# Two-pass matmul order inside a weight chunk: all leading-bit matmuls before the trailing-bit ones

## The chip, the cores and the metric

The kernel runs on one core of a Trainium2 chip. The metric is the time of one execution on the device, in microseconds, as the median over several runs. Besides this time there is one profiled execution with a trace, whose instructions can be read one by one.

## The reference

Two transformer blocks with batch 1, 256 tokens and model width 2048, in float32. Cut to what matters here, they are a chain of large matrix products with small attention, convolution and normalisation steps between them:

```python
# first block (16 meta tokens are put in front: 272 rows)
proj = rmsnorm(h, g_pre_mix) @ w_in            # 2048 -> 5382
y    = concat(fox_attention, diff_attention, conv_branch)
h    = h + rmsnorm(y @ w_out, g_post_mix)
g    = causal_dwconv(hn @ w_gate, w_conv)      # 2048 -> 5632
h    = h + rmsnorm((silu(g) * (hn @ w_up)) @ w_down, g_post_ffn)
# second block (256 rows)
z    = rms_norm(r, g_mix) @ w_in               # 2048 -> 10240
y_conv = (c_b * causal_depthwise_conv(c_c * c_x, w_conv)) @ w_conv_out
r    = r + (sigmoid(g_a) * (attn @ w_attn_out) + sigmoid(g_c) * y_conv) @ w_o
r    = r + square(relu(rms_norm(r, g_mlp) @ w_up)) @ w_down    # 2048 -> 8192 -> 2048
r    = r + sigmoid(rms_norm(r, g_ple) @ w_ple_gate) * (p @ w_ple_proj)
```

## The kernel before

Every float32 operand is split into a leading part (rounded to the matmul's short float format) and a trailing part (the rest). A product of two operands is then three short products: leading x leading, leading x trailing and trailing x leading. Activations `xs` hold both parts side by side, so that a weight tile's leading part `wh` can meet both activation parts in one matmul of 512 columns when there are 256 tokens (`both` in the code, the line of `o2`, L250). With 258 or 272 tokens two matmuls are needed for it (L252 and L253). The trailing part `wl` of the weight tile meets only the leading activations (L254, 256 to 272 columns). Below, a matmul with `wh` is called a leading matmul and one with `wl` a trailing matmul.

`chunks` (L226) walks over one product's weights. A group is `nt` blocks of 128 output columns (mostly 4), each summed up in a PSUM bank of its own over all rows of the weight. The rows come in chunks of `ck` blocks of 128 rows (4 when `nt` is 4): a chunk is one DMA of 1 MB into a `wst` buffer (3 of these), and two halves, each split by ScalarE into a `wh` tile (L158, 4 buffers) and by VectorE into a `wl` tile (L159, 3 buffers). A chunk with `nt` = 4 has 16 leading and 16 trailing matmuls. In a group's last chunk the loop goes bank by bank, and after a bank's last matmul `evac` reads the bank out: into SBUF, or added to a sum there.

The split of chunk n+1 is written ahead of the matmuls of chunk n (`queue`, `sync`). The instructions of each engine are then put into their final order by the tile framework's scheduler, with semaphores for the dependencies; on the chip each engine takes its own instructions in that order. Since there are three `wl` buffers and two per chunk, the second `wl` of chunk n+1 goes into the buffer of the first `wl` of chunk n, and waits until that one has been read for the last time.

The deque `mm` holds the banks that groups take in turn: four at first, then 5 or 6 (`N.banks(5)`, `N.banks(6)`). With six, a group's third bank is the first bank of the group before, and its fourth the second one. The read-outs that the prediction speaks of are: `evac_r` (L1163) and `evac_f_` (L974), two VectorE additions from the bank for each bank (L1168, L1169; L981, L982), after every group of the two down products and of `w_o`; `total` (L301), a ScalarE copy and a VectorE addition (L303, L304), after up, gate and input products; and `evac_cb` (L1109), `total` and seven more VectorE operations (L1117 to L1121 and a split).

Of the kernel before, what the change touches and what calls it, by code (L numbers as in the profile page):

```python
# [16 lines left out]
P = 128  # L17
# [29 lines left out]
class Net:  # L47
# [178 lines left out]
    def chunks(self, W, c0, nt, rows, xs, n, evac, x0=0, ahead=None, ck=None, merge=True):  # L226


        nc = self.nc
        both = merge and 2 * n <= 512  # L230
        cols = nt * P
        ck = ck or 2048 // cols
        nk = len(rows)
        ps = []

        def use(parts, done, c):
            if not ps:
                ps.extend(self.bank(self.mm) for _ in range(nt))
            last = done + c == nk
            for k, j in [(k, j) for j in range(nt) for k in range(c)] if last else [(k, j) for k in range(c) for j in range(nt)]:  # L240
                wh, wl, i = parts[k]
                kk = done + k
                a = rows[kk][1]
                s = slice(j * P, (j + 1) * P)
                o = ps[j][:, :n]
                st, sp = kk == 0, kk == nk - 1
                xh = xs[:, a, 0, x0:x0 + n]
                if both:
                    o2 = ps[j].rearrange("p (s n) -> p s n", s=2)[:, :, :n]
                    nc.tensor.matmul(o2, wh[:, i, s], xs[:, a, :, x0:x0 + n], start=st, stop=False)  # L250
                else:
                    nc.tensor.matmul(o, wh[:, i, s], xh, start=st, stop=False)  # L252
                    nc.tensor.matmul(o, wh[:, i, s], xs[:, a, 1, x0:x0 + n], start=False, stop=False)  # L253
                nc.tensor.matmul(o, wl[:, i, s], xh, start=False, stop=sp)  # L254
                if last and k == c - 1:
                    evac(j, o, ps[j][:, 256:256 + n] if both else None)

        done = 0
        while done < nk:
            c = min(ck, nk - done)  # L260
            while rows[done + c - 1][0] - rows[done][0] != c - 1:
                c -= 1
            w = ahead.popleft() if ahead else self.load(W, rows[done][0], c, c0, cols)
            hk = max(1, 1024 // cols)
            parts = []
            for k0 in range(0, c, hk):
                kn = min(hk, c - k0)
                wh, wl = self.split_w(w[:, k0:k0 + kn])
                parts += [(wh, wl, i) for i in range(kn)]
            yield lambda parts=parts, done=done, c=c: use(parts, done, c)  # L270
            done += c
# [1000 lines left out]
```

## Time and profile before

| what | value |
|---|---|
| time, median of 3 runs | 2668.92 us (2668.3 to 2670.02) |
| time of the profiled execution | 2666.8 us |
| its span, first to last instruction | 2665.1 us |
| TensorE busy | 2642.2 us, 99% |
| VectorE busy | 1880.6 us, 71% |
| ScalarE busy | 1308.6 us, 49% |
| DMA, share of 16 engines | about 55% on the weights' queue |
| granted TensorE clock | 1.0 of full speed over the whole span |

The span lies 1.7 us below the time of the same execution, and that execution 2.1 us below the median. A matmul's own duration in the trace includes its way through the array, which overlaps with the next matmul; how fast matmuls follow one another is read from the distance of their starts.

### The profile page before, as it was taken

How to read it: one execution, taken by the hardware profiler on the slowest of the kernel's cores; microseconds unless marked ns; L12 is line 12 of the kernel's file. 1: busy time of each engine (PE TensorE's matmuls, PEld its weight loads, DVE VectorE, ACT ScalarE, POOL GpSimd, SP SyncE). 2: the span in 40 equal slices, each digit the busy share in tenths (PEclk: the TensorE clock that was granted, in tenths of full speed). 3: DMA queues.
4: the chain of work that ended last, by engine and by line, in shares of the span. 5: the costliest groups of instructions: out<-in, count | busy, mean ns of one | idle time of the engine just before them, and what ended most of it. 6: DMA issues, size and time to landing. Idle time of an engine off the chain costs nothing.

```text
span 2665.1 us, 41518 instructions
## 1 busy us (share of the span) xinstructions
PE 2642.2 (99%) x16542; PEld 2368.7 (89%) x16542; DVE 1880.6 (71%) x3460; ACT 1308.6 (49%) x2018; POOL 23.4 (1%) x49
## 2 busy tenths in 40 slices
PE   8999999999999999999999999999999999999999
PEld 8999999999898989888888888888888888888887
DVE  5897878866767676778766766666666666666684
ACT  5454555554444444456554555554544444444463
POOL 2000000000000000000000000000000000000000
PEclk9999999999999999999999999999999999999999
DMA  6644446555555555556445555555655665556564
GB/s 211 181 148 143 131 137 199 180 183 189 190 190 188 179 188 189 178 176 204 154 160 179 177 185 189 190 190 177 191 192 191 188 190 192 190 188 190 193 216 152
DMA packets 275586, 483.63 MB, mean 181 GB/s; under 512 B 8528, under 2 KB 75025, under 8 KB 275248
## 3 DMA queue, kind: packets, MB, share of 16 engines
q1 hardware_dynamic: 272560, 475.83, 55.0%
q8 instruction: 130, 2.13, 0.3%
q0 software_dynamic: 1680, 3.18, 0.3%
q10 hardware_dynamic: 1152, 1.97, 0.2%
q14 instruction: 64, 0.52, 0.1%
HBM read 476.74 MB, written 4.20 MB: 180 GB/s over the span
## 4 chain that ended last, share of the span: by engine, by line
PE 97%; DVE 2%; DMA 0%; issue 0%; ACT 0%; SPq 0%; DVEq 0%; ACTq 0%
PE ps L250 45%; PE ps L254 31%; PE ps L252 8%; PE ps L253 7%; PE ps L288 1%; PE ps L289 1%; PE ps L287 1%; DVE wl L159 1%; PE ps L633 1%; PE ps L619 0%; PE ps L626 0%; DMA tok<-in_x_dram 0%; PE ps L723 0%; PE ps L1052 0%; PE ps L661 0%
## 5 line engine op out<-in xcount | busy, mean ns | idle before, releaser
L159 DVE TENSOR_TENSOR wl<-w,wh 128x1024 fp32r<-128x1024 f32 x898 | 1095.8, 1221 | 549.4 <-PE ps L254 491.3
L158 ACT ACTIVATE wh<-w 128x1024 fp32r<-128x1024 f32 x898 | 945.3, 1059 | 1039.2 <-PE ps L250 702.4
L254 PE MATMUL ps<-x,wl 128*128 128x256 f32 (+2 forms) x4400 | 1235.2, 282 | 3.5 <-DVE wl L159 3.4
L250 PE MATMUL ps<-x,wh 128*128 128x512 f32 x3008 | 1058.1, 396 | 2.9 <-DVE x L162 2.3
L254 PEld LDWEIGHTS ps<-x,wl 128*128 128x128 f32 x4400 | 831.3, 189 | 7.1 <-DVE wl L159 6.1
L250 PEld LDWEIGHTS ps<-x,wh 128*128 128x128 f32 x3008 | 563.7, 188 | 133.3 <-DVE x L162 2.5
L250 PE MATMUL ps<-hid,wh 128*128 128x512 f32 x1728 | 599.9, 391 | 0.0
L254 PE MATMUL ps<-hid,wl 128*128 128x256 f32 x1728 | 483.8, 280 | 0.0
L252 PE MATMUL ps<-x,wh 128*128 128x258 f32 (+1 forms) x1392 | 400.1, 288 | 1.8 <-ACT x L161 1.8
L253 PE MATMUL ps<-x,wh 128*128 128x258 f32 (+1 forms) x1392 | 399.0, 287 | 0.0
L250 PEld LDWEIGHTS ps<-hid,wh 128*128 128x128 f32 x1728 | 323.2, 187 | 70.8
L254 PEld LDWEIGHTS ps<-hid,wl 128*128 128x128 f32 x1728 | 326.5, 189 | 0.3
L252 PEld LDWEIGHTS ps<-x,wh 128*128 128x128 f32 x1392 | 262.4, 189 | 4.2 <-ACT x L161 2.0
L253 PEld LDWEIGHTS ps<-x,wh 128*128 128x128 f32 x1392 | 264.1, 190 | 0.6 <-DVE x L162 0.2
L254 PE MATMUL ps<-y,wl 128*128 128x258 f32 (+1 forms) x512 | 144.3, 283 | 0.8 <-DVE wl L159 0.8
L304 DVE TENSOR_TENSOR t<-ps,t 128x256 f32<-128x256 f32 x160 | 67.6, 422 | 44.8 <-ACT t L303 43.6
L254 PEld LDWEIGHTS ps<-y,wl 128*128 128x128 f32 x512 | 97.0, 190 | 1.9 <-DVE wl L159 1.0
L250 PE MATMUL ps<-y,wh 128*128 128x512 f32 x256 | 90.9, 399 | 0.0
L250 PE MATMUL ps<-m,wh 128*128 128x512 f32 x256 | 90.5, 399 | 0.0
L303 ACT ACTIVATE t<-ps 128x256 f32<-128x256 f32 x160 | 60.3, 377 | 59.2 <-PE ps L254 59.2
L1168 DVE TENSOR_TENSOR h<-ps,h 128x256 f32<-128x256 f32 x144 | 61.0, 423 | 36.9 <-PE ps L254 34.0
L491 DVE SCALAR_TENSOR_TENSOR scr<-scr,par 128x258 f32<-128x258 f32 x180 | 82.5, 479 | 1.2
(255 smaller groups left out, 2037.7 us busy)
## 6 DMA issues: line engine op xcount, KB each, us to landing
w<-in_w_in_dram SPq DMA_DIRECT2D x117, 1024.0 KB, 5.2
w<-in_w_down_dram SPq DMA_DIRECT2D x108, 1024.0 KB, 5.1
w<-in_w_up_dram SPq DMA_DIRECT2D x106, 1024.0 KB, 5.5
w<-in_w_gate_dram SPq DMA_DIRECT2D x44, 1024.0 KB, 5.2
w<-in_w_o_dram SPq DMA_DIRECT2D x16, 1024.0 KB, 5.1
w<-in_w_ple_gate_dram SPq DMA_DIRECT2D x16, 1024.0 KB, 5.3
w<-in_w_out_dram SPq DMA_DIRECT2D x12, 1024.0 KB, 5.1
w<-in_w_attn_out_dram SPq DMA_DIRECT2D x8, 1024.0 KB, 5.0
```

Of the source, the lines that this page charges most:

```text
L158: nc.scalar.activation(hi, src, AF.Copy)
L159: return nc.vector.tensor_tensor(lo, src, hi.bitcast(F32), ALU.subtract)
L250: nc.tensor.matmul(o2, wh[:, i, s], xs[:, a, :, x0:x0 + n], start=st, stop=False)
L252: nc.tensor.matmul(o, wh[:, i, s], xh, start=st, stop=False)
L253: nc.tensor.matmul(o, wh[:, i, s], xs[:, a, 1, x0:x0 + n], start=False, stop=False)
L254: nc.tensor.matmul(o, wl[:, i, s], xh, start=False, stop=sp)
L287: self.nc.tensor.matmul(ps[b], xh, wh[:, j], start=k == 0, stop=False)
L288: self.nc.tensor.matmul(ps[b], xh, wl[:, j], start=False, stop=False)
L303: self.nc.scalar.activation(out, b, AF.Copy)
L304: self.nc.vector.tensor_tensor(out, a, out, ALU.add)
L491: V.scalar_tensor_tensor(cv[:, c], src, wdw_col(k, c), cv[:, c], ALU.mult, ALU.add)
L1168: V.tensor_tensor(r[:, i], ps2, r[:, i], ALU.add)
```

## The change

Within a chunk the loop is cut in two. First all leading matmuls of the chunk run, always row block by row block with the banks inside. Then all trailing matmuls run, in the same order, or, in a group's last chunk, bank by bank with the read-out behind each bank. Number, shapes and operands of the matmuls stay as they are, and so do buffers, banks, splits and loads. `gemm_rows` and the attention's own matmuls are not touched.

```diff
             last = done + c == nk
-            for k, j in [(k, j) for j in range(nt) for k in range(c)] if last else [(k, j) for k in range(c) for j in range(nt)]:
-                wh, wl, i = parts[k]
+
+            order = [(k, j) for k in range(c) for j in range(nt)]
+            for k, j in order:
+                wh, _, i = parts[k]
                 kk = done + k
                 a = rows[kk][1]
-                s = slice(j * P, (j + 1) * P)
-                o = ps[j][:, :n]
-                st, sp = kk == 0, kk == nk - 1
-                xh = xs[:, a, 0, x0:x0 + n]
+                lhs = wh[:, i, j * P:(j + 1) * P]
                 if both:
                     o2 = ps[j].rearrange("p (s n) -> p s n", s=2)[:, :, :n]
-                    nc.tensor.matmul(o2, wh[:, i, s], xs[:, a, :, x0:x0 + n], start=st, stop=False)
+                    nc.tensor.matmul(o2, lhs, xs[:, a, :, x0:x0 + n], start=kk == 0, stop=False)
                 else:
-                    nc.tensor.matmul(o, wh[:, i, s], xh, start=st, stop=False)
-                    nc.tensor.matmul(o, wh[:, i, s], xs[:, a, 1, x0:x0 + n], start=False, stop=False)
-                nc.tensor.matmul(o, wl[:, i, s], xh, start=False, stop=sp)
+                    o = ps[j][:, :n]
+                    nc.tensor.matmul(o, lhs, xs[:, a, 0, x0:x0 + n], start=kk == 0, stop=False)
+                    nc.tensor.matmul(o, lhs, xs[:, a, 1, x0:x0 + n], start=False, stop=False)
+            for k, j in [(k, j) for j in range(nt) for k in range(c)] if last else order:
+                _, wl, i = parts[k]
+                kk = done + k
+                o = ps[j][:, :n]
+                nc.tensor.matmul(o, wl[:, i, j * P:(j + 1) * P], xs[:, rows[kk][1], 0, x0:x0 + n], start=False, stop=kk == nk - 1)
                 if last and k == c - 1:
                     evac(j, o, ps[j][:, 256:256 + n] if both else None)
```

The scheduler answers to the new order, also on engines whose code is unchanged. The first place is TensorE between two groups of the last down product. `ps3488` to `ps3491` are the banks of the ending group, `ps3502` to `ps3505` those of the next; `ps3504` lies in the bank of `ps3488`, `ps3505` in that of `ps3489`. Before:

```order
L250 MATMUL ps3491_22700<-hid3001_19332,wh3486_22693 128x512
L254 MATMUL ps3491_22700<-hid3001_19332,wl3487_22694 128x256
L250 MATMUL ps3502_22793<-hid3001_19332,wh3493_22735 128x512 [waits Activation_49]
L254 MATMUL ps3502_22793<-hid3001_19332,wl3494_22736 128x256 [waits DVE_49]
L250 MATMUL ps3503_22794<-hid3001_19332,wh3493_22735 128x512 [waits PE_49]
L254 MATMUL ps3503_22794<-hid3001_19332,wl3494_22736 128x256
L250 MATMUL ps3504_22795<-hid3001_19332,wh3493_22735 128x512 [waits DVE_49,PE_49]
L254 MATMUL ps3504_22795<-hid3001_19332,wl3494_22736 128x256
L250 MATMUL ps3505_22796<-hid3001_19332,wh3493_22735 128x512 [waits DVE_49,PE_49]
```

The same place of the change:

```order
L258 MATMUL ps3491_22700<-hid3001_19332,wl3485_22690 128x256 x2
L258 MATMUL ps3491_22700<-hid3001_19332,wl3487_22694 128x256 x2
L249 MATMUL ps3502_22793<-hid3001_19332,wh3493_22735 128x512 [waits Activation_49]
L249 MATMUL ps3503_22794<-hid3001_19332,wh3493_22735 128x512 [waits PE_49]
L249 MATMUL ps3504_22795<-hid3001_19332,wh3493_22735 128x512 [waits DVE_49,PE_49]
L249 MATMUL ps3502_22793<-hid3001_19332,wh3493_22735 128x512
L249 MATMUL ps3503_22794<-hid3001_19332,wh3493_22735 128x512
L249 MATMUL ps3504_22795<-hid3001_19332,wh3493_22735 128x512
L249 MATMUL ps3502_22793<-hid3001_19332,wh3495_22739 128x512 [waits Activation_49]
L249 MATMUL ps3505_22796<-hid3001_19332,wh3493_22735 128x512 [waits DVE_49,PE_49]
```

Before, the fourth bank's first matmul is the seventh of the new group; now it is the eighth, behind seven leading matmuls, since the scheduler has put three others ahead of it. The last trailing matmul with `wl3485`, the ending chunk's first `wl`, is now the third from the chunk's end.

The second place is VectorE at the same boundary. `wl3494` and `wl3496` are the two trailing halves of the next group's first chunk, and `wl3496` goes into the buffer of `wl3485`. Before:

```order
L159 TENSOR_TENSOR wl3494_22736<-w3492_22733,wh3493_22735 128x1024 [waits DMAHW5_49,PE_49,Activation_49]
L1168 TENSOR_TENSOR h_135<-ps3488_22697,h_135 128x256 [waits PE_49]
L1169 TENSOR_TENSOR h_135<-ps3488_22697,h_135 128x256 [waits DVE_49]
L1168 TENSOR_TENSOR h_135<-ps3489_22698,h_135 128x256 [waits PE_49]
L1169 TENSOR_TENSOR h_135<-ps3489_22698,h_135 128x256 [waits DVE_49]
L1168 TENSOR_TENSOR h_135<-ps3490_22699,h_135 128x256 [waits PE_49]
L1169 TENSOR_TENSOR h_135<-ps3490_22699,h_135 128x256 [waits DVE_49]
L159 TENSOR_TENSOR wl3496_22740<-w3492_22733,wh3495_22739 128x1024 [waits PE_49,Activation_49]
L1168 TENSOR_TENSOR h_135<-ps3491_22700,h_135 128x256 [waits PE_49]
```

The same place of the change:

```order
L159 TENSOR_TENSOR wl3494_22736<-w3492_22733,wh3493_22735 128x1024 [waits DMAHW5_49,PE_49,Activation_49]
L1172 TENSOR_TENSOR h_135<-ps3488_22697,h_135 128x256 [waits PE_49]
L1172 TENSOR_TENSOR h_135<-ps3489_22698,h_135 128x256 [waits PE_49]
L1173 TENSOR_TENSOR h_135<-ps3488_22697,h_135 128x256 [waits DVE_49]
L159 TENSOR_TENSOR wl3496_22740<-w3492_22733,wh3495_22739 128x1024 [waits PE_49,Activation_49]
L1173 TENSOR_TENSOR h_135<-ps3489_22698,h_135 128x256 [waits DVE_49]
L1172 TENSOR_TENSOR h_135<-ps3490_22699,h_135 128x256
L1172 TENSOR_TENSOR h_135<-ps3491_22700,h_135 128x256 [waits PE_49]
```

Before, the read-outs of three banks stand ahead of the waiting split `wl3496`; now the second bank's last read (`L1173` of `ps3489`) stands behind it.

The third place is VectorE after the first `evac_cb` group of the convolution. `wl2424` is the second trailing half of the next group's first chunk, `wl2435` and `wl2437` those of its second chunk. The piece of the change, with 19 rows left out:

```order
L159 TENSOR_TENSOR wl2424_15430<-w2420_15423,wh2423_15429 128x1024 [waits DVE_49,PE_49]
L1123 SCALAR_TENSOR_TENSOR t2426_15456<-scr2286_14701,par_106,t2426_15456 128x256 [waits DVE_49]
...
L1123 SCALAR_TENSOR_TENSOR t2432_15501<-scr2286_14701,par_106,t2432_15501 128x256 [waits DVE_49]
L159 TENSOR_TENSOR wl2435_15512<-w2433_15509,wh2434_15511 128x1024 [waits DMAHW4_49]
L159 TENSOR_TENSOR y1944_13068<-t2430_15486,y1944_13068 128x256 [waits Activation_49]
L1124 TENSOR_TENSOR t2432_15501<-t2432_15501,rB1939_13045 128x256 [waits DVE_49]
L159 TENSOR_TENSOR wl2437_15516<-w2433_15509,wh2436_15515 128x1024 [waits PE_49]
```

Between `wl2424` and `wl2435` stand 21 instructions now, and 15 before.

## Rows read from the trace of the kernel before

**Rows 1.** Page, parts 1 and 4: busy time, and the chain by line.

```profile
PE 2642.2 (99%) x16542; PEld 2368.7 (89%) x16542; DVE 1880.6 (71%) x3460; ACT 1308.6 (49%) x2018; POOL 23.4 (1%) x49
PE ps L250 45%; PE ps L254 31%; PE ps L252 8%; PE ps L253 7%; PE ps L288 1%; PE ps L289 1%; PE ps L287 1%; DVE wl L159 1%; PE ps L633 1%; PE ps L619 0%; PE ps L626 0%; DMA tok<-in_x_dram 0%; PE ps L723 0%; PE ps L1052 0%; PE ps L661 0%
```

**Rows 2.** Page, part 5: leading matmuls of 512 columns; xcount | busy, mean ns | idle.

```profile
L250 PE MATMUL ps<-x,wh 128*128 128x512 f32 x3008 | 1058.1, 396 | 2.9 <-DVE x L162 2.3
L250 PE MATMUL ps<-hid,wh 128*128 128x512 f32 x1728 | 599.9, 391 | 0.0
```

**Rows 3.** Who TensorE waited for: total us, times, longest us.

```profile
PE ps L254 <- DVE wl L159: 4.1, 5, 1.4
```

**Rows 4.** Busy time by stretch; in brackets the count of instructions.

```profile
1440.00:1860.00 420.00, 418.64 (x2370) 362.61 (x2369) 276.31 (x417) 211.66 (x308) 0.00 (x0) 1.00 0.56 184
1880.00:2560.00 680.00, 680.00 (x3925) 599.57 (x3924) 465.55 (x701) 328.11 (x455) 0.00 (x0) 1.00 0.60 192
```

**Rows 5.** Timeline of TensorE, `gemm_rows`: start us, duration us (17 rows between).

```profile
2629.83 0.39 PE L288 MATMUL ps<-wl,x 128*128 128x512 f32 x1
...
2633.91 0.39 PE L288 MATMUL ps<-wl,x 128*128 128x512 f32 x1
```

**Rows 6.** Timeline of TensorE, matmuls of 256 columns (9 rows between).

```profile
425.55 0.28 PE L829 MATMUL ps<-wl,pl 128*128 128x256 f32 x1
...
426.74 0.28 PE L830 MATMUL ps<-wh,pl 128*128 128x256 f32 x1
```

**Rows 7.** Timeline of TensorE where 512-column matmuls follow pairs (6 rows between).

```profile
2568.16 0.28 PE L254 MATMUL ps<-hid,wl 128*128 128x256 f32 x1
2568.28 0.39 PE L287 MATMUL ps<-wh,x 128*128 128x512 f32 x1
...
2569.90 0.40 PE L288 MATMUL ps<-wl,x 128*128 128x512 f32 x1
```

**Rows 8.** Timeline of TensorE, runs of one kind in the touched loop.

```profile
1203.86 1.58 PE L250 MATMUL ps<-x,wh 128*128 128x512 f32 x6
...
1496.32 1.08 PE L250 MATMUL ps<-x,wh 128*128 128x512 f32 x4
1498.76 0.74 PE L254 MATMUL ps<-x,wl 128*128 128x256 f32 x4 [1.36 <-DVE wl L159]
```

**Rows 9.** Timeline of TensorE and VectorE, a matmul and the read-out it releases.

```profile
2134.14 0.28 PE L254 MATMUL ps<-hid,wl 128*128 128x256 f32 x1
...
2134.45 0.42 DVE L1168 TENSOR_TENSOR h<-ps,h 128x256 f32<-128x256 f32 x1 [0.50 <-PE ps L254]
2134.91 0.43 DVE L1169 TENSOR_TENSOR h<-ps,h 128x256 f32<-128x256 f32 x1
```

**Rows 10.** Timeline of TensorE and VectorE, a matmul and the split it releases.

```profile
2085.60 0.28 PE L254 MATMUL ps<-x,wl 128*128 128x256 f32 x1
...
2085.98 1.23 DVE L159 TENSOR_TENSOR wl<-w,wh 128x1024 fp32r<-128x1024 f32 x1 [1.53 <-PE ps L254]
```

**Rows 11.** Timeline of VectorE, splits and read-outs after one another.

```profile
2135.25 1.22 DVE L159 TENSOR_TENSOR wl<-w,wh 128x1024 fp32r<-128x1024 f32 x1
2136.39 0.42 DVE L1168 TENSOR_TENSOR h<-ps,h 128x256 f32<-128x256 f32 x1
2136.72 1.22 DVE L159 TENSOR_TENSOR wl<-w,wh 128x1024 fp32r<-128x1024 f32 x1
```

**Rows 12.** Timeline of VectorE and the weight loads (PEld): a late split.

```profile
1497.49 1.22 DVE L159 TENSOR_TENSOR wl<-w,wh 128x1024 fp32r<-128x1024 f32 x1
...
1498.76 0.54 PEld L254 LDWEIGHTS ps<-x,wl 128*128 128x128 f32 x4 [1.79 <-DVE wl L159]
```

**Rows 13.** Timeline of VectorE after the first `evac_cb` group; and TensorE there.

```profile
1425.69 0.42 DVE L159 TENSOR_TENSOR y<-t,y 128x256 fp32r<-128x256 f32 x1
...
1430.88 1.21 DVE L159 TENSOR_TENSOR wl<-w,wh 128x1024 fp32r<-128x1024 f32 x1
...
1432.14 0.74 PE L254 MATMUL ps<-x,wl 128*128 128x256 f32 x4 [0.53 <-DVE wl L159]
```

## The prediction

> **What bounds the kernel now.** I read the page first. TensorE is busy for 2642.2 of 2665.1 us, and the chain of work that ended last lies on it for 97%, almost all in the touched loop [rows 1]. VectorE and ScalarE have room on average, so a change of order on TensorE can move the time in three ways only: by how closely matmuls follow each other, by the waits of TensorE that exist, and by waits that it makes. The list of waits shows how few there are: the trailing matmuls waited five times for a late VectorE split, 4.1 us in all [rows 3]. Then I looked at the rhythm, by stretches without other work on TensorE. From 1880 to 2560 us 3925 matmuls take 680 us, 0.3465 us for a pair of a leading and a trailing one; from 1440 to 1860 it is 2370 in 420 us, of which 1.4 is a wait, so 0.3533 a pair [rows 4, 8]. The granted clock is 1.00, the 2.4 GHz level, in both [rows 4]. So the same pair has two rhythms, 0.0068 us apart, and the slower one costs 1185 x 0.0068 = 8 us in that stretch alone.
>
> **The change, term by term.** No matmul, weight load, split or transfer is added or removed. What moves is the order on TensorE and, through the scheduler, that of VectorE.
>
> *Rhythm.* In a row, 512-column matmuls follow at (2633.91 - 2629.83)/18 = 0.2267 us [rows 5] and 256-column ones at (426.74 - 425.55)/10 = 0.119 us [rows 6]. Sixteen of each, a chunk of four banks, take 3.63 + 1.90 = 5.53 us, as the fast rhythm does (16 x 0.3465 = 5.54) and 0.12 us less than the slow one. That is the gain if rows of one kind always run so: 8 us, and I allow 2 more for stretches that I did not separate. Against it stands that a row of 512-column matmuls that follows pairs does not start at this rhythm: its first seven steps take 1.62 us, 0.231 each, 0.033 us more than seven at 0.2267 [rows 7]. The touched loop has 5248 such pairs (3008 and 1728 [rows 2] and 512 with other operands by the code), that is 328 chunks, so a start like this in each would cost 328 x 0.033 = 11 us. The short runs of leading matmuls that the loop has already say both: six at (1.58 - 0.40)/5 = 0.236, four at (1.08 - 0.40)/3 = 0.227 [rows 8]. Bounds: -10 and +11. I take -5: the run that touched the slow stretch came at 0.227, and the start's price falls mostly where now the fast rhythm rules.
>
> *Five late splits.* Leading matmuls now give 3.63 us of cover before a chunk's first trailing one. That is more than the longest of the five waits, 1.4 us [rows 3]. Three go: 4.1 less the two after `evac_cb`, 0.53 and 1.36 [rows 13, 8], which I cost below, -2.2 us.
>
> *Banks at a group's end.* The four banks of a group used to finish 4 pairs apart, 1.39 us; now four trailing matmuls apart, 0.48 us, all in the last 1.9 us of the chunk. I walk one boundary of the last down product with the order above; zero is the end of the group's last matmul slot. The last reader of the ending chunk's first `wl` starts three slots earlier, at -0.36. A split starts 0.38 after the start of the matmul that releases it (2085.60 to 2085.98 [rows 10]): at +0.02. The instruction behind it starts 1.14 later (2135.25 to 2136.39 [rows 11]): the second bank's last addition at +1.16, and it ends 0.42 later [rows 9] at +1.58. A weight load that waited for VectorE starts 0.05 after its end (1497.49 + 1.22 = 1498.71 to 1498.76 [rows 12]): +1.63. The matmul that needs this bank stands behind seven leading ones, at 7 x 0.2267 = +1.59. Its weight load would start 0.12 earlier to keep the rhythm, at +1.47: 0.16 us late. The wait holds up every matmul behind it, so it is on the path. Groups with two additions as read-out are 20 of the first down product, 32 of the second and 4 of `w_o` by the code; I count 54 boundaries, +8 us. After groups read out by `total` the matmul stands behind nine (2.04) and the read-out comes one operation later (+1.16 + 0.33 + 0.42 + 0.05 = +1.96 against 1.92): 0.04 us at some 30 places, +1.5 with the few gate products that are shorter. Behind gate groups both banks are read ahead of the split: nothing. These prices hang on tenths of a microsecond: if the walk is 0.16 too slow it is 0 (and no gain, since these banks are not waited for now); if it is 0.16 too fast, it is +22.
>
> A rule bears on this term. The Trainium skill, page "TensorE: Matmul & The Clock Gate", part 2, says that TensorE pulls weight loads ahead of matmuls still in flight. By it the load would already lie in the array when the bank comes free, the loss would shrink from 0.16 to 0.04 a boundary, and the term from 8 to 2 us. The row speaks against it: the weight load starts only when VectorE is done, and its matmul with it [rows 12].
>
> *Convolution.* After an `evac_cb` group VectorE has 21 instructions between two splits, 15 before; the 15 took 1430.88 - 1425.69 = 5.19, 0.346 each [rows 13]. From the waiting split at +0.02: 1.14 + 21 x 0.346 = the next split at +8.4, its end at +9.6. The second chunk's trailing matmuls come at 5.54 + 3.63 = +9.2, their load at 9.05: 0.6 late, and the other half, three instructions later, is 0.8 late again. Two groups at 1.4 make 2.8 against 1.9 now, +1; and some 1 us for bank waits at the four other groups with five banks, worked out as above. Together +2, from 0 to +5.
>
> *Ends of stages.* Where a stage ends on its last read-out, the fourth bank's is released at the same moment as now, but three others stand close ahead of it. At most three additions of 0.34 us at four places, +4; I take 0, since the read-outs that I walked keep up but for the split between them.
>
> *Sum.* -5 - 2.2 + 8 + 1.5 + 2 = +4.3 us. The profiled execution took 2666.8 us; the median of the runs is 2668.92, and I add to it: 2673 us.
>
> **Rivals.**
>
> *The rhythm comes back in full and the banks come in time* (faster). One mechanism: rows of one kind lock at 0.2267 and 0.119 from their first matmul, -10, and the slots in which the scheduler put the fourth bank's matmul hold. For it: a long row runs without any deviation [rows 5]. It decides if the walk is 0.1 us too slow. With the late splits 2669 - 10 - 2 = 2657 us, or 2653 if the convolution gains too.
>
> *Banks cost more and each run pays its start* (slower). The start of 0.033 in each chunk is +11, banks at 0.3 us a boundary +16: 2669 + 11 + 16 - 2 = 2694 at its end, 2680 with half of it. For it: the run of six at 0.236 [rows 8], and a boundary that has no slack in the walk. Against: 256-column rows step at 0.119, a trifle below 0.120, which may give some back [rows 6].
>
> *Nothing visible happens.* The rhythm keeps its two levels in the new order, and the scheduler's slots cover the banks: 2669 - 2 = 2667 us. That the order itself stays as it was is excluded by the rows of the order above. The skill's rule on loads pulled ahead, with the rhythm unchanged, would end here too: 2669 + 2 + 2 - 2 = 2671.
>
> **How the numbers follow.** Of this kernel a measurement can tell about 0.2%, 5.3 us, from no change: 2663.6 to 2674.3. The forecast has 0.45, with its own range of 2665 to 2681, so that it lies about half below and half above the upper bound; the faster rival 0.20, the slower one 0.25, nothing visible 0.10. Faster by over 0.2%: the faster rival and a little of the forecast, 0.22. Within: half of the forecast, nothing visible and some of the slower rival, 0.36. Slower: 0.42. The range reaches from the faster rival's 2656 to 2688, between the two values of the slower one.
>
> **What would show it.** Right: no wait of trailing matmuls for splits but after `evac_cb`; waits of leading matmuls for VectorE's second addition, some fifty of 0.1 to 0.2 us; the stretch of `w_o` and the products before it nearer to 0.3465 us a pair than to 0.3533. Wrong: the last down product at 0.3465 with no such waits (banks in time), or a stretch without waits slower than 0.3533 a pair (the start of each run is dear). A third case would be VectorE splits late on a chunk's leading side, which I have excluded since ScalarE's `wh` buffers come free earlier than now.

## The result, and the profile of the changed kernel

| | kernel before | changed kernel |
|---|---|---|
| median of 6 runs each, taken side by side, us | 2668.61 (2661.26 to 2670.02) | 2682.44 (2678.85 to 2686.14) |
| ratio, 95% interval | | 1.0055 [1.0045, 1.0065] |
| span of the profiled execution, us | 2665.1 | 2682.5 |
| its own time, us | 2666.8 | 2684.47 |

The change costs 13.8 us by the medians, a ratio of 1.0055. That is above what a measurement here can tell from no change, and the kernel is slower, the way that was forecast; the forecast time, 2673, is 9 us short.

The page of the changed kernel, parts 1 and 4, answers to [rows 1]: TensorE has the same 16542 matmuls and is the chain as before.

```profile
PE 2655.5 (99%) x16542; PEld 2375.5 (89%) x16542; DVE 1824.6 (68%) x3460; ACT 1306.9 (49%) x2020; POOL 23.3 (1%) x49
...
PE ps L249 44%; PE ps L258 28%; PE ps L252 6%; PE ps L253 6%; PE ps L292 1%; PE ps L293 1%; PE ps L291 1%; DVE wl L159 1%; DMA w<-in_w_out_dram 1%; PE ps L637 1%; ACT wh L158 0%; PE ps L623 0%; PE ps L630 0%; DVE rB L863 0%; DMA w<-in_w_up_dram 0%
```

The list of waits of TensorE in the changed kernel (total us, times, longest us) answers to [rows 3]:

```profile
PE ps L343 <- DVE rB L863: 3.0, 2, 1.8
...
PE ps L252 <- DVE m L870: 2.6, 1, 2.6
...
PE ps L258 <- DVE wl L159: 2.2, 4, 0.6
```

The trailing matmuls (now L258) wait four times for a late split, 2.2 us, and all four follow `evac_cb` groups. Waits for `rB`, the last sum at the end of a stage, are 3.0 us; in the list of the kernel before they are 0.5:

```profile
PE ps L339 <- DVE rB L859: 0.5, 1, 0.5
```

The wait of 2.6 us (L252) is taken up below.

The same stretches as in [rows 4], busy time and in brackets the count of instructions (a count has some two matmuls in it that began ahead of the stretch):

```profile
1440.00:1860.00 420.00, 417.85 (x2393) 366.15 (x2392) 270.72 (x430) 209.44 (x308) 0.00 (x0) 1.00 0.56 188
1880.00:2560.00 680.00, 680.00 (x3876) 592.68 (x3876) 432.49 (x673) 321.61 (x443) 0.00 (x0) 1.00 0.59 190
```

From 1880 to 2560 us there are now 3876 matmuls, where there were 3925; from 1440 to 1860 us 2393, where there were 2370. So the change gained where pairs were slow and lost more where they were fast. Both kernels have 16542 matmuls, so the start of the k-th one can be compared across traces. This table gives by how many us each kernel's profiled execution falls behind that of the kernel before within each stretch (stretches by the times of before, the last 95 us left out; the kernels of the last five columns are described below):

| stretch, us | what runs there | changed | pairs in the last chunk | 7 banks | 4 `wl`, 3 `wh` | mixed | before, four more times |
|---|---|---|---|---|---|---|---|
| 0 to 387 | first block's attention | +0.5 | +1.4 | +0.5 | -0.6 | -0.6 | -0.8 to +0.4 |
| 387 to 480 | `w_out`, stage end | +7.5 | +1.9 | +3.2 | +1.5 | +1.5 | -0.4 to +0.9 |
| 480 to 1150 | first FFN | +2.8 | +0.4 | +3.0 | -1.6 | -1.6 | 0 to +0.1 |
| 1150 to 1425 | stage end, attention | +2.7 | +1.8 | +3.5 | +4.1 | +5.1 | +1.4 to +3.2 |
| 1425 to 1530 | convolution | +0.1 | -2.2 | +0.1 | -2.6 | -2.6 | -1.1 to 0 |
| 1530 to 1869 | merge, `w_o` | -5.2 | -3.8 | -5.9 | -5.9 | -5.7 | 0 |
| 1869 to 2564 | second FFN | +8.9 | +8.0 | +3.0 | +3.0 | +0.2 | 0 |

The last column is needed to read the others: the profiled execution of before that the prediction used was 1.4 to 3.2 us ahead of four later ones of the same kernel between 1150 and 1425 us. So the +2.7 there lies within what this kernel does without the change. Of the +7.5 from 387 to 480 us some 4 us begin with a load of `w_out` that landed late in this execution. The waits between 390 and 403 us say so,

```profile
ACT wh L158 <- DMA w<-in_w_out_dram: 3.5, 1, 3.5
```

and the stretches behind it (the last three figures are granted clock, DMA share and GB/s) show what followed.

```profile
397.00:400.00 3.00, 0.84 (x7) 0.62 (x6) 1.90 (x4) 1.38 (x3) 0.00 (x0) 0.99 0.00 0
400.00:404.00 4.00, 3.61 (x19) 3.61 (x20) 2.57 (x6) 1.81 (x3) 0.00 (x0) 0.58 0.46 104
404.00:410.00 6.00, 6.00 (x53) 6.00 (x52) 2.95 (x4) 1.01 (x3) 0.00 (x0) 1.00 0.62 232
```

TensorE stood from about 397.8 to 400.4 us and then got 0.58 of its clock for 4 us, which is the 1.2 GHz level for most of it. With seven banks, a kernel that does not differ from the changed one up to the merge, this stretch cost 3.2.

A lower clock is not a matter of this one execution, though. As a mean over the run it was 0.996 to 0.998 in the six runs of the changed kernel, and 0.998 to 1.000 in all runs of the kernel before for which the record lists it. The six times go with it: 2678.85 and 2680.41 us at 0.998, 2681.84 to 2684.47 at 0.997, 2686.14 at 0.996.

### The profile page after: what moved, and what is told of

It is laid out like the page before. It is cut to its first block, busy times and chain, and to the rows that moved or that the text cites. A ratio compares the mean times of both kernels' runs of the same rounds, so it can differ in the third digit from the quotient of the medians.

```text
span 2682.5 us, 41595 instructions
## 1 busy us (share of the span) xinstructions
PE 2655.5 (99%) x16542; PEld 2375.5 (89%) x16542; DVE 1824.6 (68%) x3460; ACT 1306.9 (49%) x2020; POOL 23.3 (1%) x49
## 4 chain that ended last, share of the span: by engine, by line
PE 91%; DVE 3%; DMA 1%; ACT 1%; issue 0%; DVEq 0%; ACTq 0%; SPq 0%
PE ps L249 44%; PE ps L258 28%; PE ps L252 6%; PE ps L253 6%; PE ps L292 1%; PE ps L293 1%; PE ps L291 1%; DVE wl L159 1%; DMA w<-in_w_out_dram 1%; PE ps L637 1%; ACT wh L158 0%; PE ps L623 0%; PE ps L630 0%; DVE rB L863 0%; DMA w<-in_w_up_dram 0%
## 5 line engine op out<-in xcount | busy, mean ns | idle before, releaser
L159 DVE TENSOR_TENSOR wl<-w,wh 128x1024 fp32r<-128x1024 f32 x898 | 1078.0, 1219 | 389.2 <-issue 180.9
L249 PE MATMUL ps<-x,wh 128*128 128x512 f32 x3008 | 733.0, 394 | 3.3 <-DVE x L162 2.3
L258 PE MATMUL ps<-x,wl 128*128 128x256 f32 (+2 forms) x4400 | 579.1, 283 | 2.2 <-DVE wl L159 2.2
L258 PEld LDWEIGHTS ps<-x,wl 128*128 128x128 f32 x4400 | 563.3, 190 | 19.8 <-DVE wl L159 3.4
L249 PE MATMUL ps<-hid,wh 128*128 128x512 f32 x1728 | 420.7, 393 | 0.3 <-DVE m L986 0.3
L252 PE MATMUL ps<-x,wh 128*128 128x258 f32 (+1 forms) x1392 | 351.3, 289 | 1.9 <-ACT x L161 1.8
L253 PE MATMUL ps<-x,wh 128*128 128x258 f32 (+1 forms) x1392 | 346.1, 286 | 0.1
L252 PEld LDWEIGHTS ps<-x,wh 128*128 128x128 f32 x1392 | 264.9, 190 | 5.6 <-issue 2.1
L258 PEld LDWEIGHTS ps<-hid,wl 128*128 128x128 f32 x1728 | 221.6, 191 | 8.6
L258 PE MATMUL ps<-hid,wl 128*128 128x256 f32 x1728 | 224.2, 283 | 0.0
L1172 DVE TENSOR_TENSOR h<-ps,h 128x256 f32<-128x256 f32 x144 | 57.6, 420 | 83.8 <-PE ps L258 81.8
L258 PE MATMUL ps<-y,wl 128*128 128x258 f32 (+1 forms) x512 | 68.9, 284 | 0.0
L252 PE MATMUL ps<-y,wh 128*128 128x258 f32 x256 | 65.9, 291 | 2.8 <-DVE m L870 2.6
L258 PEld LDWEIGHTS ps<-y,wl 128*128 128x128 f32 x512 | 65.4, 190 | 1.7 <-issue 0.4
L253 PE MATMUL ps<-y,wh 128*128 128x258 f32 x256 | 65.4, 291 | 0.0
L985 DVE TENSOR_TENSOR m<-ps,m 128x256 f32<-128x256 f32 x80 | 31.9, 420 | 48.3 <-PE ps L258 47.2
```

Source lines behind the costliest of these rows:

```text
L159: return nc.vector.tensor_tensor(lo, src, hi.bitcast(F32), ALU.subtract)
L249: nc.tensor.matmul(o2, lhs, xs[:, a, :, x0:x0 + n], start=kk == 0, stop=False)
L252: nc.tensor.matmul(o, lhs, xs[:, a, 0, x0:x0 + n], start=kk == 0, stop=False)
L253: nc.tensor.matmul(o, lhs, xs[:, a, 1, x0:x0 + n], start=False, stop=False)
L258: nc.tensor.matmul(o, wl[:, i, j * P:(j + 1) * P], xs[:, rows[kk][1], 0, x0:x0 + n], start=False, stop=kk == nk - 1)
L985: V.tensor_tensor(fo[:, i], ps2, fo[:, i], ALU.add)
```

## The experiments

**Pairs again in the last chunk, and the reverse.** Two kernels that each keep half of the change: passes in all chunks but the last of a group, and passes in the last chunk alone.

```
+            bank = [(k, j) for j in range(nt) for k in range(c)]
+            order = [(k, j) for k in range(c) for j in range(nt)]
+            if not last:              # second kernel: if last
+                seq = [(0, k, j) for k, j in order] + [(1, k, j) for k, j in (bank if last else order)]
+            else:
+                seq = [(t, k, j) for k, j in (bank if last else order) for t in (0, 1)]
...
```

Here 0 is a leading and 1 a trailing matmul.

Expected of the first: 

> Edit: the two passes stay in a group's chunks but the last; the last chunk goes back to pairs, bank by bank. Theory A (two prices of the new order: a start of 0.019 us in every chunk, and waits for banks that come free together at a group's end and at a stage's end, together some 14 us; a gain of 5 to 6 us where the pairs ran at 0.3533): the bank waits go, the gain stays in some 62 of 88 chunks of the slow stretch (-4 to -5), the start price in 80 chunks of the second FFN (+1.5) and about as much in the first block: 2664 to 2669 us, at or below the kernel before. Rival B (the start of each run is the main price, or each change of kind costs, and the banks hardly wait): most of the 13.8 us stays, about 2676. Rival C (the time goes at the ends of stages by a shift of VectorE's order alone): between, about 2672.

Expected of the second: 

> Edit: two passes in a group's last chunk alone, all other chunks in pairs as before the change. Theory A: bank waits and stage ends cost what they cost in the whole change (+14 us), the gain of the slow stretch comes only in 26 of 88 chunks (-1.5), start prices in some 110 chunks at most (+1): 2680 to 2686 us, no better than the whole change. Rival B (starts dear, banks cheap): about a third of the price, 2671 to 2674. Rival C (VectorE's order at stage ends): about 2677.

Measured: 2672.04 us, ratio 1.0021 [1.0012, 1.0030], and 2701.36 us, ratio 1.0131 [1.0113, 1.0148]. The first is 10 us better than the whole change, so most of the price sits in the last chunks. But it missed theory A's 2664 to 2669, and its second FFN shows why:

```profile
1880.00:2560.00 680.00, 680.00 (x3880) 595.38 (x3880) 451.24 (x685) 316.44 (x446) 0.00 (x0) 1.00 0.60 191
```

There are no bank waits left, and still 3880 matmuls. In the trace the pairs of every last chunk there repeat the steps 233, 117, 241, 120, 236, 113 ns, 0.3533 us a pair. In the kernel before, pairs of the same operands at the same place step 230, 117, 230, 117, 0.3467 a pair. So the slow rhythm is not bound to the stretch where I had found it. 48 last chunks x 16 x 0.0066 = 5.1 us of the +8.0 are this. The rest is the start of runs: a chunk of passes behind slow pairs takes 0.056 us more than sixteen fast pairs, 47 of them 2.6 us, and one behind other passes 0.020, 33 of them 0.7 us.

The second kernel was 15 us above the upper end of theory A's range. TensorE's wait for splits between 1420 and 1540 us, around the convolution, is alone

```profile
PE ps L254 <- DVE wl L159: 7.1, 2, 4.0
```

longer than all such waits in the kernel before or in the changed one. Its other losses (+8.4 us in the first FFN, +12.9 in the second) fit bank waits as in the whole change and slow pairs, but I did not take them apart, nor did I find why the convolution's two waits grew so long.

**Runs half as long.** As the first kernel above, but a chunk goes as 8 leading, 8 trailing, 8 leading, 8 trailing.

```
+                hk = max(1, 1024 // cols)
+                seq = []
+                for k0 in range(0, c, hk):
+                    seq += [(t, k, j) for t in (0, 1) for k, j in order if k0 <= k < k0 + hk]
```

Expected: 

> Edit: as the kernel with pairs in the last chunk, but the other chunks go in two halves: 8 leading, 8 trailing, 8 leading, 8 trailing. It doubles the number of run starts and changes nothing else. Theory A (0.019 us for each start of a leading run after a trailing one, once per run): some 200 more starts, +3 to +4 us against the kernel with whole runs, and in the stretches without other work 0.038 us a chunk more than sixteen fast pairs. Rival B (the price belongs to the chunk, its first weight load of a new tile): no difference to that kernel, within 1 us. Rival C (half the run is enough for the slow pairs' gain or not): the stretch from 1440 to 1860 us falls back towards 0.3533 a pair, +3 us there alone.

Measured: 2676.16 us, ratio 1.0038 [1.0024, 1.0052], 4.1 above the kernel with whole runs (medians), as theory A had it; the second FFN takes 0.95 us more for 80 more starts. By chunk, one behind other passes now takes 0.040 us more than sixteen fast pairs where it took 0.020, so a second start costs as much as the first; one behind slow pairs takes 0.063 where it took 0.056. The price belongs to the start of a run, not to the chunk.

**One more buffer for the split.** The changed kernel with four `wl` and three `wh` buffers.

```
-        self.whp = pool("whp", 4)
-        self.wlp = pool("wlp", 3)
+        self.whp = pool("whp", 3)
+        self.wlp = pool("wlp", 4)
```

Expected: 

> Edit: the changed kernel with four buffers instead of three for VectorE's splits (wl) and three instead of four for ScalarE's (wh), which keeps the memory. The split that stands between VectorE's read-outs of a group no longer waits for the trailing matmuls of the chunk that just ends. Theory A (a group's fourth bank is late because that split holds the read-outs up): the bank waits of the second FFN vanish, some 5 us there and 1 to 3 in the first FFN; 2674 to 2677 us if three wh buffers suffice. Rival B (the read-outs are late by their own length, four of them after 1.9 us): nothing moves, 2682. Rival C (three wh buffers are too few: leading matmuls now wait for ScalarE): slower, above 2690, with waits of the leading matmuls for ScalarE in the list.

Measured: 2665.72 us, ratio 1.0002 [0.9993, 1.0012]: 16.7 us below the changed kernel, level with the kernel before. The waits for banks are gone, and more than theory A had for them. First the changed kernel at one boundary of the second FFN, VectorE (DVE), TensorE (PE) and its weight loads (PEld), in order of time:

```profile
2068.13 3.37 PE L249 MATMUL ps<-hid,wh 128*128 128x512 f32 x13
...
2068.16 1.23 DVE L159 TENSOR_TENSOR wl<-w,wh 128x1024 fp32r<-128x1024 f32 x1
...
2069.30 0.42 DVE L1173 TENSOR_TENSOR h<-ps,h 128x256 f32<-128x256 f32 x1
...
2069.64 0.75 DVE L1172 TENSOR_TENSOR h<-ps,h 128x256 f32<-128x256 f32 x2
2069.83 1.45 PEld L249 LDWEIGHTS ps<-hid,wh 128*128 128x128 f32 x7 [0.35 <-issue]
2070.30 0.74 DVE L1173 TENSOR_TENSOR h<-ps,h 128x256 f32<-128x256 f32 x2
...
2070.96 1.22 DVE L159 TENSOR_TENSOR wl<-w,wh 128x1024 fp32r<-128x1024 f32 x1
```

The group's last matmul slot ends at 2068.13. The split (L159) begins at 2068.16, when the ending chunk's `wl` comes free. Behind it the second bank's last addition (L1173) starts at 2069.30 and ends at 2069.72; the weight load of the matmul that needs this bank starts at 2069.83, after 0.35 us of idleness. The steps of the leading matmuls there are 348 and 307 ns instead of 227. Now the same kind of boundary with four `wl` buffers:

```profile
2064.44 0.74 DVE L1173 TENSOR_TENSOR h<-ps,h 128x256 f32<-128x256 f32 x2
2064.86 3.36 PE L249 MATMUL ps<-hid,wh 128*128 128x512 f32 x14
2065.10 0.75 DVE L1172 TENSOR_TENSOR h<-ps,h 128x256 f32<-128x256 f32 x2
2065.76 0.75 DVE L1173 TENSOR_TENSOR h<-ps,h 128x256 f32<-128x256 f32 x2
2066.43 1.22 DVE L159 TENSOR_TENSOR wl<-w,wh 128x1024 fp32r<-128x1024 f32 x1
```

VectorE reads all banks first (L1172, L1173) and the split comes at 2066.43, behind them; nothing on TensorE waits. And by stretches:

```profile
1440.00:1860.00 420.00, 419.93 (x2412) 370.59 (x2410) 275.44 (x425) 212.83 (x312) 0.00 (x0) 1.00 0.58 191
1880.00:2560.00 680.00, 680.00 (x3913) 601.10 (x3913) 448.47 (x696) 321.87 (x448) 0.00 (x0) 1.00 0.60 192
```

3913 matmuls in the second FFN against 3925 before: what is left is the start of each run. By the k-th matmul this kernel loses 0.40 us for each 640 matmuls there, evenly, which are 20 chunks: 0.020 us a chunk.

**The same exchange in the kernel before.** Expected: 

> Edit: the kernel before with the same exchange of buffers, four for wl and three for wh. It tells whether the exchange alone pays. Theory A (the exchange mends what the new order broke, bank waits of a split that stands between read-outs): the kernel before has no such waits, so only its late splits go, up to 4 us: 2664 to 2668 us, and the new order with the exchange is no better than this. Rival B (the exchange pays by itself, the order does not matter): about 17 us faster, 2651. Rival C (pairs need four wh buffers, since a wh tile is held until the chunk's last pair): slower, above 2675, with waits of leading matmuls for ScalarE.

Measured: 2679.6 us, ratio 1.0063 [1.0040, 1.0086]: rival C. The exchange does not pay by itself. TensorE's waits in this kernel:

```profile
PE ps L254 <- DVE wl L159: 3.2, 5, 0.7
...
PE ps L252 <- ACT wh L158: 2.1, 2, 1.6
```

Pairs hold a `wh` tile until the chunk's end, so with three of them ScalarE comes late (L252). Some 5 us are lost up to 480 us and 5.5 between 1150 and 1425, of which 1.4 to 3.2 also come without an edit; the waits in the list are a small part of this, and the rest was not traced. In the new order a `wh` tile is free after the leading half of a chunk. Either edit alone is slower than the kernel before; together they are level with it.

**Seven banks.** The other way to take the wait away: the changed kernel with another bank.

```
-    N.banks(6)
+    N.banks(7)
     ms = N.pairs(SEQ, "m")
```

Expected: 

> Edit: the changed kernel with seven banks instead of six for products from the merge of the second block on (the other uses of the matmul memory keep one). A group's fourth bank is then one that the group before has read out first. Theory A (the fourth bank's late read-out is the wait): it goes without any change of VectorE's order, 5 to 6 us of the second FFN's 8 and 1 to 2 in the merge; 2674 to 2677 us. Rival B (VectorE's split is late in itself and holds later things up, and the bank is only where it shows): the wait moves to the trailing matmuls, less than 2 us gained, 2680 to 2682. Rival C (one bank for the rest makes the work between stages queue up): the end of the kernel gets longer by a few us.

Measured: 2674.01 us, ratio 1.0030 [1.0020, 1.0041], 8.4 us below the changed kernel; theory A. Its row for the second FFN

```profile
1880.00:2560.00 680.00, 680.00 (x3910) 601.04 (x3909) 440.41 (x691) 326.14 (x452) 0.00 (x0) 1.00 0.60 192
```

agrees with that of the four `wl` buffers, and the table above gives +3.0 for both. Two edits that share nothing but the bank wait leave the same rest, so the wait's size is the difference: 8.9 - 3.0 = 5.9 us in the second FFN. The wait itself stands in the list of weight loads that stood idle in the changed kernel from 1880 to 2560 us; with seven banks there is no such entry:

```profile
PEld ps L249 <- issue: 9.7, 29, 0.4
```

**Is the slow rhythm a matter of the place?** The kernel before, with transposes that nothing reads put between two groups at 14 places.

```
+        def f():
+            ps = N.aux()
+            with N.behind(N.tail):          # behind the last trailing matmul
+                for _ in range(n):
+                    PE.transpose(ps[:, :P], ident, ident)
```

Expected: 

> Edit: the kernel before, with 1 to 4 transposes of 128 columns, which nothing reads, put between two groups at 14 places: once in each of the four rounds of the merge (after the first gate group), three times in the w_o product, and behind the up products of seven of the second FFN's eight steps. No other matmul moves. Theory A (the two rhythms of pairs are states into which TensorE falls when a row of pairs begins, and which it keeps until something comes between; they belong to no stage): between two such places all pairs run at 0.3467 or all at 0.3533 us, some of the pieces from 1499 to 1861 us come out fast, some of the second FFN may come out slow; the time moves by up to 7 us either way, by 0.0066 us for each pair that changed. Rival B (the slow rhythm belongs to the operands or to the other engines' work of that stretch): every piece of it stays at 0.3533 and every piece of the second FFN at 0.3467, and the kernel is slower by the transposes alone, some 35 at 0.1 us, 3 to 4 us.

Measured: 2681.5 us, ratio 1.0059 [1.0042, 1.0076]. Stretches between two such places, four of the merge (60 us each) and four of the second FFN (80 us each):

```profile
1525.00:1585.00 60.00, 60.00 (x342) 52.03 (x341) 37.35 (x54) 29.34 (x42) 0.00 (x0) 1.00 0.58 197
1592.00:1652.00 60.00, 60.00 (x348) 52.96 (x347) 38.41 (x55) 30.18 (x43) 0.00 (x0) 1.00 0.58 199
1660.00:1720.00 60.00, 60.00 (x342) 52.09 (x341) 37.41 (x54) 29.35 (x42) 0.00 (x0) 1.00 0.57 191
1727.00:1787.00 60.00, 60.00 (x341) 52.11 (x340) 37.89 (x54) 29.63 (x42) 0.00 (x0) 1.00 0.55 189
1955.00:2035.00 80.00, 80.00 (x455) 69.43 (x454) 50.91 (x73) 33.23 (x41) 0.00 (x0) 1.00 0.58 185
2045.00:2125.00 80.00, 80.00 (x455) 69.47 (x454) 51.34 (x74) 33.79 (x42) 0.00 (x0) 1.00 0.59 189
2135.00:2215.00 80.00, 80.00 (x464) 70.60 (x463) 52.08 (x74) 34.68 (x43) 0.00 (x0) 1.00 0.60 192
2225.00:2305.00 80.00, 80.00 (x455) 69.35 (x454) 51.38 (x74) 33.56 (x41) 0.00 (x0) 1.00 0.58 187
```

With two matmuls off each count, 340 in 60 us are 0.3529 a pair and 346 are 0.3468; 453 in 80 us are 0.3532 and 462 are 0.3463. Each piece is of one kind from end to end. The second piece of the merge turned fast, the third slow again; the second FFN, fast in the kernel before, is slow in three of the four pieces shown. The same operands and the same neighbours run at either pace: rival B is out. The pace changes at a few transposes and then holds for up to 256 pairs. Of the fourteen pieces behind transposes three ran fast, of the seven in the second FFN one. Their number does not choose it (behind two of them came a fast piece in the merge, a slow one in the second FFN). The kernel lost 14 us where theory A allowed 7: some 1480 pairs of the second FFN that turned slow are about 10 us, and 35 transposes at 0.109 us are 4.

**The kernel before, four more times.** Expected of the second and third profile: 

> No edit: the kernel before, profiled once more. Its runs lie in two heaps, at 2660 to 2664 and at 2668 to 2670 us. Theory A (the state of pairs between 1432 and 1861 us is drawn anew in each execution): 1206 pairs at 0.0066 us are 8.0 us, so an execution of the lower heap shows that stretch at 0.3467 a pair, and one of the upper heap at 0.3533. Rival B (the two heaps are the clock's fall at the end of the first block's FFN, or waits elsewhere): the stretch is at 0.3533 in both, and the difference stands elsewhere. For the fall of the granted clock near 1200 us, which the changed kernel shows and the first profile of before does not: if it belongs to the order, this profile shows 1.00 there as well; if to the execution, it may fall here too.

> No edit: the kernel before, profiled a third time, with the same expectations as the profile before this: the lower heap of its times goes with pairs at 0.3467 in the stretch from 1432 to 1861 us if the state is drawn in each execution, and the fall of the granted clock near 1200 us comes and goes with the execution if it does not belong to the order.

Expected of the fourth and fifth: 

> No edit: the kernel before, profiled a fourth time, since the second and third fell into the upper heap of its times. Theory A (state of pairs drawn when a row of pairs begins): if the run falls into the lower heap, below 2664 us, the 1026 pairs from about 1500 to 1862 us run at 0.3467, 6.8 us less than in the first profile; in the upper heap they run at 0.3533. Rival B: in a run of the lower heap that stretch still stands at 0.3533 and the difference lies elsewhere.

> No edit: the kernel before, profiled a fifth time, with the same expectations: below 2664 us goes with 0.3467 us a pair from 1500 to 1862 us if the state of pairs is what parts the two heaps, and with 0.3533 if something else does.

Measured: 2667.84, 2669.47, 2670.1 and 2668.77 us, all in the upper group. Two stretches of the second profile

```profile
1440.00:1495.00 55.00, 55.00 (x314) 47.71 (x313) 33.70 (x51) 24.10 (x31) 0.00 (x0) 1.00 0.57 187
1195.00:1200.00 5.00, 4.65 (x25) 4.02 (x26) 5.00 (x10) 2.56 (x5) 0.00 (x0) 1.00 0.48 163
```

and of the third:

```profile
1440.00:1495.00 55.00, 55.00 (x319) 48.48 (x318) 33.79 (x49) 23.67 (x30) 0.00 (x0) 1.00 0.61 205
1195.00:1200.00 5.00, 3.40 (x12) 2.83 (x13) 5.00 (x11) 3.72 (x7) 0.52 (x1) 0.74 0.48 147
```

One program, and from 1440 to 1495 us 314 matmuls in one execution and 319 in the other: pace is set anew in each execution. From 1510 to 1860 us all four had 1983, the slow pace, so what parts the lower group from the upper was not caught: the 1026 pairs of that stretch would give 1026 x 0.0066 = 6.8 us, which fits, but no run shows it. The granted clock near 1200 us was 1.00 once and fell to 0.74 or 0.66 in the other three, so a fall there does not need the new order. How low the clock is over a run does go with the order of the last chunk: its mean over the runs on record is 0.9987 to 0.9992 in the five kernels that have pairs there, 0.9963 to 0.9984 in the five that have passes there (the mixture below up to the second FFN); it is 0.9991 in the kernel before and 0.9972 in the changed one. Single runs are listed to 0.001.

**A mixture.** The new order with four `wl` and three `wh` buffers up to the second FFN, pairs from there.

```
+            if self.two:
+                seq = [(0, k, j) for k, j in order] + [(1, k, j) for k, j in (bank if last else order)]
+            else:
+                seq = [(t, k, j) for k, j in (bank if last else order) for t in (0, 1)]
...
+    N.two = False
     chunks = [list(range(c, c + 8)) for c in range(0, NF2, 8)]
```

Expected: 

> Edit: new order with four wl and three wh buffers up to the second FFN, pairs as before the change from there. Theory A (the new order with those buffers costs 0.020 us a chunk where pairs run at 0.3467, and saves where they run at 0.3533; the second FFN's pairs begin at 0.3467 in every kernel so far): 128 chunks less of 0.020, 2.5 us below the kernel with those buffers throughout, 2663 us, some 4 to 5 below the kernel before's median; the second FFN's matmuls stand as far apart as in the kernel before. Rival B (the row of pairs begins in the other state this time): 2048 pairs at 0.3533, 11 us above the kernel with those buffers throughout, 2677. Rival C (three wh buffers make pairs wait there): a few us with waits for ScalarE in the list.

Measured: 2663.49 us, ratio 0.9983 [0.9974, 0.9992], 4.9 below the kernel before in the same comparison (2668.42): the fastest of all, and at theory A's 2663. Its second FFN

```profile
1880.00:2560.00 680.00, 680.00 (x3925) 599.60 (x3924) 463.83 (x699) 327.20 (x452) 0.00 (x0) 1.00 0.60 194
```

has the 3925 matmuls of the kernel before. The faster runs of the kernel before, 2660 to 2664 us, are as fast as this one.

## Why the prediction was right, and where its sum fell short

The measured 2682 us lies in the stated range, which ends at 2688, but 1 us above the forecast's own part of it (2665 to 2681), and close to the slower rival with half of its price (2680). The sign and the wait that makes it were right; the gain and loss together were forecast at +4.3 us and measured at 13.8.

**Rhythm, -5.** The size was right, half of the reason wrong. Without bank waits the new order gains 5.9 us from 1530 to 1869 us and 1.6 in the first FFN (0.5 of it a late split) and loses 3.0 in the second, -4.5. The loss is the start of each run, 0.020 us a chunk against the 0.033 that I bounded it with. But I took the slow pace for a property of the stretch. It is set when a row of pairs begins, it differs between executions, and the new order takes away the chance of the fast pace along with the risk of the slow one.

**Late splits, -2.2.** Right: no trailing matmul waits but after `evac_cb`.

**Banks, +9.5.** The mechanism was right, and it is the term that decides the sign. The walk put the second addition at +1.16, its end at +1.58 and the weight load at +1.63 behind the last slot; the rows above give +1.17, +1.59 and +1.70. Measured against the kernel with seven banks, four successive boundaries of the last product cost 0.15, 0.24, 0.21 and 0.21 us (0.16 in the walk), those behind `total` 0.01 to 0.02 (0.04). The walk gives 32 x 0.16 + 16 x 0.04 = 5.8 for the second FFN, and 5.9 was lost there; that these agree so closely is luck, since 29 boundaries waited, at 0.20, and those behind `total` cost almost nothing. Behind a wait the row also starts anew (steps of 224 to 236 ns), which the walk left out. Another 0.7 was lost in merge and `w_o`, and 4.4 in the first FFN (2.8 + 1.6, from the kernel with four `wl` buffers, if all that the buffers bring there is the bank wait): 11.0 in all. The 54 boundaries at 0.16 are 8.6 in the forecast, not 8.

The rule that I weighed against it, that weight loads are pulled ahead of matmuls in flight (the Trainium skill, "TensorE: Matmul & The Clock Gate", part 2), would have made 2 us of these by my estimate. For a load that waits for another engine this trace shows no pulling ahead: it began at 2069.83, 0.11 us after the addition's end, and its matmul 0.03 behind it.

**Convolution, +2.** Too much: 0.1 measured. Four waits came, as forecast, but 2.2 us instead of 2.8, and no bank waits that can be seen beside them.

**Ends of stages, 0.** This is the term that failed. I let them pass because the read-outs that I had walked keep up. But the last sum of a stage (`rB`) waits for all four read-outs, and these now end together: TensorE waits for it 1.2 us more at the end of `w_out` and 1.3 more at the end of the first FFN, 2.5 of the 4 that I gave as the bound. One of the late splits, 1.0 us, lay in these two stretches, so they should have come out 1.0 us ahead. Against the mean of the later profiles of before they are 2.6 behind from 387 to 480 (3.2 with seven banks against 0.6) and 0.5 behind from 1150 to 1425 (2.7 against 2.2). The rest beside the waits for `rB` is in good part the clock, which the sum did not price. The kernel before and the one with seven banks, behind the end of `w_out`:

```profile
430.00:440.00 10.00, 7.92 (x63) 7.51 (x63) 9.96 (x22) 7.21 (x16) 2.16 (x4) 1.00 0.55 197
430.00:440.00 10.00, 8.19 (x46) 7.98 (x45) 8.78 (x26) 6.94 (x14) 2.70 (x5) 0.69 0.44 163
```

With seven banks TensorE had waited 1.2 us for `rB` just before; then the granted clock was 0.69 over these 10 us, 1.2 GHz for part of them. By the k-th matmul 1.2 us were lost at the wait and 2.4 in the 12 us behind it, and 0.5 came back later. Whether such a fall comes differs between executions: it was 0.83 here in three of the later profiles of before, and 1.00 with four `wl` buffers, which waited 0.9 us for `rB`.

**The sum.** Terms as measured: -4.5 + 11.0 + 0.1 + 3.1 for the stage ends, the late splits in these stretches already off, make +9.7; the stretch before 387 us is left out. The medians differ by 13.8 with an interval of 12 to 17. The rest of some 4 us I could not place, and single profiles of one kernel differ by as much. The clock is a candidate: by the means above, 0.0019 of 2682 us, the changed kernel had some 5 us less of it, an estimate, and part of that is already in the terms. The slower rival was half right: each run does pay its start, but at 0.020, and the banks at 0.2 a boundary, not 0.3. That the array locks at 0.2267 and 0.119 from a run's first matmul, the faster rival, is refuted by the 0.40 us for each 20 chunks.

## What to carry to other kernels

When an order makes several results ready at once, walk the engine that reads them out instruction by instruction, with whatever else stands in its queue: here one split of 1.2 us between the additions made the fourth bank late at 29 boundaries of the second FFN. Then look for the buffer that puts it there; one `wl` buffer more, taken from a tile that the new order frees earlier, was worth 17 us in the new order, and cost 12 in the old one. A stage's end has no next group to hide such a bunch, so price it apart from the boundaries within.

Before a difference of pace between two stretches is put down to the stretches, put something small between two groups and look whether the pace stays.

## What the runs showed of the chip

- Pairs of a 512-column and a 256-column matmul, each with its own weight load, run at one of two paces, 0.3467 or 0.3533 us, both with the granted clock at 1.00. A row of pairs keeps the pace that it began with, for 2018 pairs in the longest case, until something comes between. It is settled at the break, and can come out differently in two executions of the same program. What in TensorE makes the two paces was not found.
- A run of sixteen 512-column matmuls behind 256-column ones starts with steps of 233, 236, 228, 233 and 230 ns and then holds 227; the sixteen 256-column ones start at 113 and hold 120. Together 0.020 us a chunk above sixteen fast pairs.
- The granted clock fell to the 1.2 GHz level behind waits at a stage's end: in the changed kernel TensorE was busy for 0.67 us from 1206 to 1209 us, and had 0.50 of its clock from 1209 to 1212. It fell in some executions and not in others of one kernel.
